# Residual loads and early stores of 4 MB instead of 2 MB, and a clear of the semaphores under the last stores, in a 3x3 convolution with a residual add

## The chip, the cores and the metric

One core of one Trainium2 chip. The metric is the device time of one execution in microseconds. A run is one execution; each comparison takes runs of both kernels in turn on the same chip.

## The reference

```python
batch, c_in, h, w, c_out, k = 16, 64, 64, 64, 64, 3
x_pad = np.pad(x, ((0, 0), (0, 0), (1, 1), (1, 1)))
for b, co, ci, kh, kw in ...:
    output[b, co] += weight[co, ci, kh, kw] * x_pad[b, ci, kh:kh+h, kw:kw+w]
return output + residual
```

`x`, `residual` and the output are 16 x 64 x 64 x 64 float32 each, 16.78 MB. An image of 64 channels fills 64 partitions, so two images, a pair, fill 128: 2.1 MB for each tensor and pair, called 2 MB here.

## The kernel before

The engines go by the names of the trace: PE is TensorE, DVE VectorE, ACT ScalarE, POOL GpSimd and SP SyncE. A DMA moves data between HBM, where the tensors lie, and SBUF, the core's working memory; PE writes its results to PSUM.

SP issues nearly all DMAs, in one order: x and residual of each pair alternately, then the stores. x comes into three buffers (`xr`), ACT casts it to bfloat16 (`xp`), PE makes 24 matmuls for each image, and DVE adds the result to the residual in place (`ro`, all eight pairs stay in SBUF). Of the eight stores six are issued inside the kernel's own block, when DVE has finished their pair; the last two come after it.

```python
    def load_ro(p):
        nc.sync.dma_start(out=ro[p][:, :], in_=res_bc[128 * p : 128 * p + 128, :]).then_inc(s_r[p], 16)
    ...
        for p in range(NPAIR):
            if p >= NXR:
                nc.sync.wait_ge(s_half, 2 * (p - NXR) + 3)        # ACT has emptied the x buffer
            if p == 0:
                to_the_front(load_x(p, cols=slice(0, NPIX // 2)))   # first half of x0, from SP
                nc.sync.dma_start(out=wraw[:, :], in_=w_rows[:, :]).then_inc(s_w, 16)
            else:
                load_x(p)
            load_ro(p)
        for p in range(NEARLY):                                     # NEARLY = 6
            nc.sync.wait_ge(s_add, 2 * p + 3)
            store(p).then_inc(s_out, 16)
    ...
        to_the_front(load_x(0, nc.scalar, slice(NPIX // 2, NPIX)))  # second half of x0, from ACT
    ...
    for p in range(NEARLY, NPAIR):
        store(p)
    with tc.tile_critical(sync_engine=mybir.EngineType.Pool, no_gpsimd_drain=True):
        nc.gpsimd.wait_ge(s_out, 16 * NEARLY)
```

Of the kernel before, what the change touches and what calls it, by code (L numbers as in the profile page):

```python
# [8 lines left out]
FP32 = mybir.dt.float32  # L9
# [6 lines left out]
def kernel(  # L16
# [7 lines left out]
    nc = tc.nc  # L24

    B, C, H, W = x.shape
# [4 lines left out]
    NPIX = H * W  # L31
    NPAIR = B // 2
# [2 lines left out]
    NCHUNK = J // JC  # L35
    NXR = 3
    NXP = 4
    NEARLY = 6

    res_bc = residual.rearrange("b c h w -> (b c) (h w)")  # L40
    out_bc = out.rearrange("b c h w -> (b c) (h w)")
    x_bc = x.rearrange("b c h w -> (b c) (h w)")
    w_rows = weight.rearrange("co (h ci) kh kw -> (co h) (ci kh kw)", h=2)

    pool = ctx.enter_context(tc.tile_pool(name="pool", bufs=1))
    psum = ctx.enter_context(tc.tile_pool(name="psum", bufs=1, space=bass.MemoryType.PSUM))

    ident = pool.tile([128, 128], FP32)
    ro = [pool.tile([128, NPIX], FP32, name=f"ro{p}") for p in range(NPAIR)]
    xr = [nc.alloc_sbuf_tensor(f"xr{i}", [128, NPIX], FP32) for i in range(NXR)]  # L50

    xp = [pool.tile([128, J + 1, W], BF16, name=f"xp{i}") for i in range(NXP)]
# [4 lines left out]
    sem = lambda name: tc.alloc_semaphore(name)  # L57
    s_w = sem("s_w")
    s_x = [sem(f"s_x{i}") for i in range(NXR)]
    s_r = [sem(f"s_r{p}") for p in range(NPAIR)]  # L60
    s_out = sem("s_out")
    s_id = sem("s_id")
    s_wt = sem("s_wt")
    s_half = sem("s_half")
    s_pack = sem("s_pack")
    s_bank = sem("s_bank")
    s_conv = sem("s_conv")
    s_add = sem("s_add")

    def load_x(p, engine=nc.sync, cols=slice(0, NPIX)):  # L70
        return engine.dma_start(out=xr[p % NXR][:, cols], in_=x_bc[128 * p : 128 * p + 128, cols]).then_inc(
            s_x[p % NXR], 16
        )

    def load_ro(p):
        nc.sync.dma_start(out=ro[p][:, :], in_=res_bc[128 * p : 128 * p + 128, :]).then_inc(s_r[p], 16)

    def store(p):
        return nc.sync.dma_start(out=out_bc[128 * p : 128 * p + 128, :], in_=ro[p][:, :])

    def matmul(out_, lhsT, rhs, start, stop, ldweights):

# [18 lines left out]
    def to_the_front(dma):  # L101



        def fixed(ap):
            t = ap.bass_ap.tensor.name
            return mybir.PhysicalAccessPattern(
                ap=ap.ap, offset=ap.bass_ap.offset, dtype=ap.dtype, memref=t, memsetref=t + "_set", bass_ap=ap.bass_ap
            )

        front = nc.main_func.blocks[0].instructions
        here = nc.cur_bb.bb.instructions
        ins = here.pop()
        assert ins.name == dma.ins.name
        at = next(
            i for i, e in enumerate(front) if e.engine == ins.engine and isinstance(e, mybir.InstDrain)
        )
        front.insert(at, copy.replace(ins, ins=[fixed(a) for a in ins.ins], outs=[fixed(a) for a in ins.outs]))
# [5 lines left out]
    def weight_block(h, half, d, par, kh):  # L124

        at = 64 * half + 32 * h
        return dict(out=wl[at : at + 32, d, :, par, :], in_=tp[0:32, kh, 0:384].rearrange("p (kw co h) -> p kw co h", kw=3, h=2)[:, :, :, h])

    with tc.tile_critical(no_gpsimd_drain=True):  # L129

        for p in range(NPAIR):
            if p >= NXR:

                nc.sync.wait_ge(s_half, 2 * (p - NXR) + 3)
            if p == 0:
                to_the_front(load_x(p, cols=slice(0, NPIX // 2)))
                nc.sync.dma_start(out=wraw[:, :], in_=w_rows[:, :]).then_inc(s_w, 16)
            else:
                load_x(p)
            load_ro(p)  # L140
        for p in range(NEARLY):
            nc.sync.wait_ge(s_add, 2 * p + 3)
            store(p).then_inc(s_out, 16)


        nc.gpsimd.memset(ident[:, :], 0.0).then_inc(s_id, 1)  # L146
        nc.gpsimd.wait_ge(s_id, 1)
        nc.gpsimd.affine_select(  # L148
            out=ident[:, :],
            in_=ident[:, :],  # L150
            compare_op=mybir.AluOpType.not_equal,
            fill=1.0,
            base=0,
            pattern=[[-1, 128]],
            channel_multiplier=1,
        ).then_inc(s_id, 1)
        nc.gpsimd.wait_ge(s_id, 2)
        for t in xp:
            nc.gpsimd.memset(t[0:64, 0, :], 0.0).then_inc(s_id, 1)  # L159
            nc.gpsimd.memset(t[64:128, J, :], 0.0).then_inc(s_id, 1)  # L160
        nc.gpsimd.memset(wl[0:64, 0, :, 1, :], 0.0).then_inc(s_id, 1)  # L161
        nc.gpsimd.memset(wl[64:128, 1, :, 0, :], 0.0).then_inc(s_id, 1)  # L162


        to_the_front(load_x(0, nc.scalar, slice(NPIX // 2, NPIX)))
        for n in range(B):
            p, im = divmod(n, 2)
            hp = slice(64 * im, 64 * im + 64)
            x4 = xr[p % NXR].rearrange("q (j two w) -> q j two w", two=2, w=W)
            t = xp[n % NXP]  # L170
            if im == 0:
                nc.scalar.wait_ge(s_x[p % NXR], 16 * (p // NXR + 1 + (p % NXR == 0)))
            i = nc.scalar.copy(out=t[64:128, 0:J, :], in_=x4[hp, :, 0, :])  # L173
            i.then_inc(s_half, 1)
            if n >= NXP:
                i._wait_ge(s_conv, n - NXP + 1)
            nc.scalar.copy(out=t[0:64, 1 : J + 1, :], in_=x4[hp, :, 1, :]).then_inc(s_pack, 1)  # L177
            if n == 0:
                nc.scalar.wait_ge(s_wt, 1)
                for b in blocks[4:]:  # L180
                    for h in range(2):
                        i = nc.scalar.copy(**weight_block(h, *b))  # L182
                i.then_inc(s_wt, 1)


        nc.vector.wait_ge(s_wt, 1)
        for k, b in enumerate(blocks[:4]):
            for h in range(2):
                i = nc.vector.tensor_copy(**weight_block(h, *b))  # L189
                if k == h == 0:  # L190
                    i.then_inc(s_bank, 2)
        i.then_inc(s_wt, 1)
        for n in range(B):
            p, im = divmod(n, 2)
            hp = slice(64 * im, 64 * im + 64)
            o4 = ro[p].rearrange("q (j two w) -> q j two w", two=2, w=W)
            psj = ps[n % 2].rearrange("q c j w -> q (c j) w")
            if im == 0:
                nc.vector.wait_ge(s_r[p], 16)
            for par in range(2):  # L200
                i = nc.vector.tensor_tensor(  # L201
                    out=o4[hp, :, par, :], in0=psj[64 * par : 64 * par + 64, :, :], in1=o4[hp, :, par, :], op=ADD
                )
                if par == 0:
                    i._wait_ge(s_conv, n + 1)

                i.then_inc(s_add if par == 0 or n == B - 1 else s_bank, 1)


        nc.tensor.wait_ge(s_id, 4 + 2 * NXP)  # L210
        nc.tensor.wait_ge(s_w, 16)
        wraw3 = wraw.rearrange("p (ci t) -> p ci t", t=9)
        for t in range(9):
            i = nc.tensor.transpose(  # L214
                out=tp[0:32, t // 3, 128 * (t % 3) : 128 * (t % 3) + 128], in_=wraw3[:, :, t], identity=ident[:, :]
            )
        i.then_inc(s_wt, 1)
        nc.tensor.wait_ge(s_wt, 3)
        with nc.Fori(0, B // NXP, 1, engines=[PE]):
            for n in range(NXP):  # L220
                nc.tensor.wait_ge(s_bank, 1).then_inc(s_bank, -1)
                nc.tensor.wait_ge(s_pack, 1).then_inc(s_pack, -1)  # L222
                order = [(1, 0), (1, 1), (0, 0), (0, 1), (2, 0), (2, 1)]
                for i, (kw, d) in enumerate(order):
                    xlo, xhi = max(0, 1 - kw), min(W, W + 1 - kw)
                    for c in range(NCHUNK):
                        j0 = JC * c
                        m = matmul(
                            ps[n % 2][:, c, :, xlo:xhi],
                            wl[:, d, kw, :, :].rearrange("q r c -> q (r c)"),  # L230
                            xp[n][:, j0 + d : j0 + d + JC, xlo + kw - 1 : xhi + kw - 1],
                            i == 0,
                            i == len(order) - 1,
                            c == 0,
                        )
                m.then_inc(s_conv, 1)


    for p in range(NEARLY, NPAIR):
        store(p)  # L240
    with tc.tile_critical(sync_engine=mybir.EngineType.Pool, no_gpsimd_drain=True):
        nc.gpsimd.wait_ge(s_out, 16 * NEARLY)


# [28 lines left out]
```

## Time and profile before

| what | value | from |
|---|---|---|
| time | 123.09 us (122.86 to 123.21, 3 runs) | the runs |
| span of the profiled run | 121.2 us | the page |
| DMA | 50.48 MB, 433 GB/s in most slices | the page |
| last add of DVE ends | 104.1 us | the timeline |
| last store has landed | 120.2 us | the landings |

The page is read with the DMA first, since those engines are the only ones busy from the first slice to the last. The prediction shows the lines. Two more are DVE's additions around image 4, in order of time: start, length of the run, how many, and in brackets how long DVE idled before it and for what.

```profile
37.27 4.61 DVE L201 TENSOR_TENSOR ro<-ps,ro 64x2048 f32<-64x2048 f32 x2 [0.58 <-PE ps L86]
42.46 4.61 DVE L201 TENSOR_TENSOR ro<-ps,ro 64x2048 f32<-64x2048 f32 x2 [0.58 <-PE ps L86]
```

Image 4, the first of pair 2, starts at 42.46 us, 0.58 us after the add before it, and what it waited for is PE.

### The profile page before, as it was taken

What the parts mean: (1) busy time and instruction counts of PE and PEld (TensorE: products, weight loads), DVE (VectorE), ACT (ScalarE), POOL (GpSimd) and SP (SyncE); (2) the same over time, 40 slices, a digit from 0 to 9 for tenths busy, and PEclk for the clock granted to TensorE, in tenths of its full rate; (3) what the DMA queues carried; (4) which work ended last, traced back from release to release, by engine and by line L of the source; (5) the groups of instructions that cost most, each with busy time, mean ns of one, the idle gap of its engine ahead of it and who ended that gap; (6) DMA issues with size and microseconds to landing.
All of it is one profiled execution on the core that took longest, in us unless ns stands there. A gap on an engine that the chain in (4) does not pass through costs nothing.

```text
span 121.2 us, 736 instructions
## 1 busy us (share of the span) xinstructions
PE 87.7 (72%) x389; PEld 10.7 (9%) x105; DVE 76.0 (63%) x40; ACT 63.1 (52%) x37; POOL 2.4 (2%) x16
## 2 busy tenths in 40 slices
PE   0033499999999999999999999999999980000000
PEld 0021001101010101010101010101010100000000
DVE  0005300889898898989889898898989889300000
ACT  4049969938966984993993994896000000000000
POOL 5200000000000000000000000000000000000000
PEclk9999999999999999999999999999999999755555
DMA  6999999999999999999999999999999999999993
GB/s 168 427 444 433 433 433 433 433 427 433 433 427 427 433 433 427 427 433 427 433 433 433 433 433 422 433 389 433 433 433 433 422 433 433 433 433 433 427 433 151
DMA packets 3744, 50.48 MB, mean 417 GB/s; under 512 B 416, under 2 KB 544, under 8 KB 544
## 3 DMA queue, kind: packets, MB, share of 16 engines
q1 hardware_dynamic: 3600, 49.43, 96.3%
q10 hardware_dynamic: 144, 1.05, 2.0%
HBM read 33.70 MB, written 16.78 MB: 417 GB/s over the span
## 4 chain that ended last, share of the span: by engine, by line
PE 71%; DVEq 2%; DVE 2%; issue 0%
PE ps L86 53%; PE ps L85 17%; DVEq L129 2%; DVE ro L201 2%
## 5 line engine op out<-in xcount | busy, mean ns | idle before, releaser
L201 DVE TENSOR_TENSOR ro<-ps,ro 64x2048 f32<-64x2048 f32 x32 | 73.2, 2289 | 17.7 <-PE ps L86 17.2
L86 PE MATMUL ps<-xp,wl 128*128 128x504 bf16 (+1 forms) x288 | 80.0, 388 | 0.2
L173 ACT CAST xp<-xr 64x2048 bf16<-64x2048 f32 x16 | 30.3, 1896 | 19.3 <-DMA xr<-in_x_dram 17.1
L85 PE MATMUL ps<-xp,wl 128*128 128x504 bf16 (+1 forms) x92 | 35.8, 389 | 3.4 <-PEq L222 3.4
L177 ACT CAST xp<-xr 64x2048 bf16<-64x2048 f32 x16 | 30.4, 1897 | 0.4
L85 PEld LDWEIGHTS ps<-xp,wl 128*128 128x128 bf16 x96 | 9.5, 99 | 79.1 <-issue 79.1
L189 DVE CAST wl<-ps 32x192 bf16<-32x192 f32 x8 | 2.8, 348 | 10.4 <-PE ps L214 10.3
L214 PE MATMUL ps<-ident,wraw 128*32 128x128 f32 x9 | 2.1, 412 | 8.1 <-DMA wraw<-in_weight_dram 8.1
L214 PEld LDWEIGHTS ps<-ident,wraw 128*32 128x32 f32 x9 | 1.2, 137 | 8.6 <-issue 8.1
L173 ACT ACT_TABLE_LOAD x1 | 1.3, 1283 | 1.1 <-SPq L129 1.1
L182 ACT CAST wl<-ps 32x192 bf16<-32x192 f32 x4 | 1.2, 306 | 0.0
L160 POOL MEMSET xp<- 64x64 bf16 x4 | 0.6, 147 | 0.2
L159 POOL MEMSET xp<- 64x64 bf16 x4 | 0.6, 145 | 0.2
L148 POOL TENSOR_SCALAR_AFFINE_SELECT ident<-ident 128x128 f32<-128x128 f32 x1 | 0.3, 295 | 0.2 <-POOL ident L146 0.2
L162 POOL MEMSET wl<- 64x192 bf16 x1 | 0.3, 253 | 0.1
L161 POOL MEMSET wl<- 64x192 bf16 x1 | 0.3, 252 | 0.1
L146 POOL MEMSET ident<- 128x128 f32 x1 | 0.2, 205 | 0.7 <-SPq L129 0.7
L257 POOL MEMSET const-uint8-127<- 128x1 uint8 x1 | 0.1, 113 | 0.0
L257 POOL MEMSET const-bfloat16-1.0<- 128x1 bf16 x1 | 0.1, 112 | 0.0
L257 POOL MEMSET const-float32-1.0<- 128x1 f32 x1 | 0.1, 109 | 0.0
L257 POOL MEMSET const-float32-0.0<- 128x1 f32 x1 | 0.1, 104 | 0.2 <-issue 0.2
## 6 DMA issues: line engine op xcount, KB each, us to landing
ro<-in_residual_dram SPq DMA_DIRECT2D x8, 2048.0 KB, 21.9
out_dram<-ro SPq DMA_DIRECT2D x8, 2048.0 KB, 28.2
xr<-in_x_dram SPq DMA_DIRECT2D x7, 2048.0 KB, 17.5
xr<-in_x_dram SPq DMA_DIRECT2D x1, 1024.0 KB, 7.0
xr<-in_x_dram ACTq DMA_DIRECT2D x1, 1024.0 KB, 7.6
wraw<-in_weight_dram SPq DMA_DIRECT2D x1, 144.0 KB, 6.9
```

Source lines behind the costliest of these rows:

```text
L85: return e.matmul(out=out_, lhsT=lhsT, rhs=rhs, start=start, stop=stop, skip_group_check=True)
L86: return e.add_instruction(mybir.InstMatmult(name=nc.get_next_instruction_name(), engine=PE, ins=[e.lower_ap(rhs), e.lower_ap(lhsT)], outs ...
L129: with tc.tile_critical(no_gpsimd_drain=True):
L159: nc.gpsimd.memset(t[0:64, 0, :], 0.0).then_inc(s_id, 1)
L160: nc.gpsimd.memset(t[64:128, J, :], 0.0).then_inc(s_id, 1)
L173: i = nc.scalar.copy(out=t[64:128, 0:J, :], in_=x4[hp, :, 0, :])
L177: nc.scalar.copy(out=t[0:64, 1 : J + 1, :], in_=x4[hp, :, 1, :]).then_inc(s_pack, 1)
L182: i = nc.scalar.copy(**weight_block(h, *b))
L189: i = nc.vector.tensor_copy(**weight_block(h, *b))
L201: i = nc.vector.tensor_tensor(out=o4[hp, :, par, :], in0=psj[64 * par : 64 * par + 64, :, :], in1=o4[hp, :, par, :], op=ADD)
L214: i = nc.tensor.transpose(out=tp[0:32, t // 3, 128 * (t % 3) : 128 * (t % 3) + 128], in_=wraw3[:, :, t], identity=ident[:, :])
L257: nc = _bacc.Bacc("TRN2", target_bir_lowering=False, num_devices=1)
```

## The change

Its intent: fewer and larger DMAs, fewer semaphores, and a clear of them while the last stores still run. (The split of the first load over both queues, which its short description also lists, is in the kernel before already.) The core of the diff:

```diff
-    NEARLY = 6
+    NEARLY = 3
+    RES = (slice(0, 1), slice(1, 2), slice(2, 4), slice(4, 6), slice(6, 8))
-    ro = [pool.tile([128, NPIX], FP32, name=f"ro{p}") for p in range(NPAIR)]
+    ro = pool.tile([128, NPAIR, NPIX], FP32)
-    s_r = [sem(f"s_r{p}") for p in range(NPAIR)]
+    s_r = [sem(f"s_r{i}") for i in range(2)]
-    s_wt = sem("s_wt")                       # its counts go to s_id
...
-    def load_ro(p):
-        nc.sync.dma_start(out=ro[p][:, :], in_=res_bc[128 * p : 128 * p + 128, :]).then_inc(s_r[p], 16)
+    def load_ro(i):
+        if i >= 2:
+            nc.sync.wait_ge(s_r[i % 2], 16 * (i // 2))
+        nc.sync.dma_start(out=ro[:, RES[i], :], in_=res_bc[:, RES[i], :]).then_inc(s_r[i % 2], 16)
...
-            load_ro(p)
-        for p in range(NEARLY):
-            nc.sync.wait_ge(s_add, 2 * p + 3)
-            store(p).then_inc(s_out, 16)
+            if p in (0, 1, 3, 5, 7):
+                load_ro((p + 1) // 2)
+        for k in range(NEARLY):
+            nc.sync.wait_ge(s_add, 4 * k + 5)
+            store(slice(2 * k, 2 * k + 2)).then_inc(s_out, 16)
...
         nc.gpsimd.wait_ge(s_out, 16 * NEARLY)
+        tc.free_semaphores([s_w, *s_x, *s_r, s_out, s_id, s_half, s_pack, s_bank, s_conv, s_add])
```

More of the change, by code (lines that the diff above doesn't have):

```diff
@@ L37 @@
     NXP = 4
-    NEARLY = 6
-    res_bc = residual.rearrange("b c h w -> (b c) (h w)")
-    out_bc = out.rearrange("b c h w -> (b c) (h w)")
+    NZERO = 4 + 2 * NXP
+    NEARLY = 3
+    RES = (slice(0, 1), slice(1, 2), slice(2, 4), slice(4, 6), slice(6, 8))
+    res_bc = residual.rearrange("(p b) c h w -> (b c) p (h w)", b=2)
+    out_bc = out.rearrange("(p b) c h w -> (b c) p (h w)", b=2)
     x_bc = x.rearrange("b c h w -> (b c) (h w)")
@@ L73, in load_x, with store @@
         )
-    def load_ro(p):
-        nc.sync.dma_start(out=ro[p][:, :], in_=res_bc[128 * p : 128 * p + 128, :]).then_inc(s_r[p], 16)
-    def store(p):
-        return nc.sync.dma_start(out=out_bc[128 * p : 128 * p + 128, :], in_=ro[p][:, :])
+    def load_ro(i):
+        if i >= 2:
+            nc.sync.wait_ge(s_r[i % 2], 16 * (i // 2))
+        nc.sync.dma_start(out=ro[:, RES[i], :], in_=res_bc[:, RES[i], :]).then_inc(s_r[i % 2], 16)
+    def store(pairs):
+        return nc.sync.dma_start(out=out_bc[:, pairs, :], in_=ro[:, pairs, :])
     def matmul(out_, lhsT, rhs, start, stop, ldweights):
@@ L178 @@
             if n == 0:
-                nc.scalar.wait_ge(s_wt, 1)
+                nc.scalar.wait_ge(s_id, NZERO + 1)
                 for b in blocks[4:]:
@@ L182 @@
                         i = nc.scalar.copy(**weight_block(h, *b))
-                i.then_inc(s_wt, 1)
-        nc.vector.wait_ge(s_wt, 1)
+                i.then_inc(s_id, 1)
+        nc.vector.wait_ge(s_id, NZERO + 1)
         for k, b in enumerate(blocks[:4]):
@@ L191 @@
                     i.then_inc(s_bank, 2)
-        i.then_inc(s_wt, 1)
+        i.then_inc(s_id, 1)
         for n in range(B):
@@ L195 @@
             hp = slice(64 * im, 64 * im + 64)
-            o4 = ro[p].rearrange("q (j two w) -> q j two w", two=2, w=W)
+            o4 = ro[:, p, :].rearrange("q (j two w) -> q j two w", two=2, w=W)
             psj = ps[n % 2].rearrange("q c j w -> q (c j) w")
             if im == 0:
-                nc.vector.wait_ge(s_r[p], 16)
+                i = next(i for i, pairs in enumerate(RES) if p < pairs.stop)
+                nc.vector.wait_ge(s_r[i % 2], 16 * (i // 2 + 1))
             for par in range(2):
@@ L207 @@
                 i.then_inc(s_add if par == 0 or n == B - 1 else s_bank, 1)
-        nc.tensor.wait_ge(s_id, 4 + 2 * NXP)
+        nc.tensor.wait_ge(s_id, NZERO)
         nc.tensor.wait_ge(s_w, 16)
@@ L216 @@
             )
-        i.then_inc(s_wt, 1)
-        nc.tensor.wait_ge(s_wt, 3)
+        i.then_inc(s_id, 1)
+        nc.tensor.wait_ge(s_id, NZERO + 3)
         with nc.Fori(0, B // NXP, 1, engines=[PE]):
@@ L236 @@
                 m.then_inc(s_conv, 1)
-    for p in range(NEARLY, NPAIR):
-        store(p)
+    for p in range(2 * NEARLY, NPAIR):
+        store(slice(p, p + 1))
     with tc.tile_critical(sync_engine=mybir.EngineType.Pool, no_gpsimd_drain=True):
         nc.gpsimd.wait_ge(s_out, 16 * NEARLY)
+        tc.free_semaphores([s_w, *s_x, *s_r, s_out, s_id, s_half, s_pack, s_bank, s_conv, s_add])
 _INS = ['x', 'weight', 'residual']
```

## The prediction

> **What bounds the kernel now.** I read the page first, its span, its slices and its DMA lines.
>
> ```profile
> span 121.2 us, 736 instructions
> DMA  6999999999999999999999999999999999999993
> ...
> DMA packets 3744, 50.48 MB, mean 417 GB/s; under 512 B 416, under 2 KB 544, under 8 KB 544
> ...
> q1 hardware_dynamic: 3600, 49.43, 96.3%
> ...
> HBM read 33.70 MB, written 16.78 MB: 417 GB/s over the span
> ...
> PE 71%; DVEq 2%; DVE 2%; issue 0%
> ```
>
> The reader is to see two things. The 16 DMA engines are busy in every slice but the first and the last. And the chain of waits (last line) names PE for 71% of the span; it misleads here, because it follows compute instructions back from the last add, and that add ends long before the span does. What ends the span is the store of the last pair. The stretches show it:
>
> ```profile
> 1.00:20.00 19.00, 8.42 (x27) 1.80 (x14) 2.78 (x8) 12.19 (x11) 2.17 (x12) 1.00 1.01 414
> 20.00:78.00 58.00, 57.84 (x267) 6.54 (x67) 50.16 (x22) 45.07 (x24) 0.00 (x0) 1.00 1.01 431
> 78.00:80.00 2.00, 2.00 (x11) 0.19 (x2) 1.42 (x2) 1.98 (x2) 0.00 (x0) 1.00 0.99 352
> 80.00:104.00 24.00, 19.43 (x90) 2.14 (x22) 21.53 (x10) 3.87 (x3) 0.00 (x0) 1.00 1.00 430
> 104.00:119.00 15.00, 0.00 (x0) 0.00 (x0) 0.13 (x1) 0.00 (x0) 0.00 (x0) 0.51 1.01 433
> 119.00:121.20 2.20, 0.00 (x0) 0.00 (x0) 0.00 (x0) 0.00 (x0) 0.00 (x0) 0.50 0.09 37
> ```
>
> Columns: the stretch, its length, busy time of PE, weight loads, DVE, ACT and POOL, granted clock, DMA share, GB/s. From 104 to 119 us no compute engine works, and the DMA engines still run at share 1.01 and 433 GB/s on stores queued before. So the end is set by bytes divided by rate.
>
> The span divides by the trace's packet and landing records like this. The first load is issued at 0.00 and its first packet starts at 1.01. Packets then run until 119.87. The last store's semaphore lands at 120.21, and the final barrier, with the clearing of semaphores, ends at 121.17. That is 1.01 + 118.86 + 0.34 + 0.96 = 121.17 us. The packets' own durations add up to 119.1 us for each of the 16 engines, so there is no idle time to win inside the 118.86: what is busy is the wire. A 16 KB packet takes 608 at best, 611 in the median and 613 ns in the mean (16 x 16,384 B / 611 ns = 429 GB/s). Only the end of an engine's list is uneven: the 16 engines finish between 119.3 and 119.9.
>
> The tail's costs, from the line of the framework's exit code, and the DMA queue's waits:
>
> ```profile
> L268 POOLq EVENT_SEMAPHORE_RANGE_CLEAR  x1: 200/200/200, 120.7 to 120.7; - x1
> ```
>
> ```profile
> SPq L71 <- ACT xp L173: 51.4, 5, 15.7
> SPq L79 <- DVE ro L201: 24.9, 4, 10.0
> SPq L129 <- DVEq L129: 17.4, 1, 17.4
> SPq L268 <- DMA out_dram<-ro: 14.8, 2, 10.0
> ```
>
> The clear is one instruction of 0.2 us. SP waits for nearly the whole span, but the DMA engines have work queued meanwhile, so these waits cost nothing.
>
> **What the Trainium skill says.** Page "DMA: Bandwidth & Descriptors", section "Where 436 GB/s comes from", gives 16 ports x 32 B x 850 MHz = 435.2 GB/s as the ceiling of one core's DMA. The trace agrees: 433 GB/s in most slices, so the steady state is within 1% of it. Section "Measured (HBM→SBUF, 128 partitions, SWDGE, issued from GpSimd)" gives 78% efficiency for 1 MB and 97% for 16 MB and advises large DMAs. That is for a transfer timed by itself; this trace doesn't agree for queued ones: its 2 MB transfers, back to back, already run at 433. Section "Why a DMA increments its semaphore by 16 and not by 1" says that each engine closes a DMA with a semaphore descriptor and that two DMAs in flight on one semaphore let a wait pass early. The trace has 416 four-byte packets, 16 for each of 26 DMAs, 9 ns each; and the second point is why the changed kernel makes SP wait before it issues a residual load on a reused semaphore. Section "Latency and other measured facts" lists row pitches of 2 MiB as slow (164 GB/s against 207 and more). In the changed kernel a partition's two rows are 2 MiB apart, but neighbouring partitions stay 16 KB apart, so I don't expect that case; no line of the kernel before tests it.
>
> **The change part by part.** The first part of its name, the load split over both queues, is in the kernel before too: both kernels issue one 1 MB half from SP and one from ACT at 0.0 and 0.13 us. Nothing moves there.
>
> (1) Residual loads go from eight of 2 MB to 2, 2, 4, 4, 4 MB, early stores from six of 2 MB to three of 4 MB. Bytes are the same and a row is still 16 KB, so the large packets are the same 2,944 of 16 KB. Six fewer DMAs (26 to 20: three loads and three stores) remove 6 x 16 = 96 semaphore packets of 9 ns over 16 engines: 96 x 9 / 16 = 54 ns. SP's six issues of about 0.43 us were hidden.
>
> (2) The order of the queue changes: x3 comes before the residual of pair 2, which now comes with pair 3's, and so on; all loads still precede all stores. I walked the queue with 4.87 us for each 2 MB (the distance of the landings before). Loads before landed at: x2 27.5, ro2 32.3, x3 37.2, ro3 42.1. After: x2 27.5, x3 32.4, residuals of pairs 2 and 3 together 42.1. DVE's first add for pair 2 (image 4) started at 42.46, so the residual arrives 0.4 us before it is needed. The next two come at 61.6 (needed at 63.2) and 81.3 (needed at 84.0). Should the first be late by d, the compute chain, where PE takes 24 matmuls x 216 ns = 5.19 us for each image with hardly any slack against DVE (2 x 2.29 us and 0.58 of wait), ends d later than 104.1.
>
> (3) Does the queue ever run dry? x5 waits for image 6's first cast, after x3: issued at about 37, while queued work reaches to 47. x7 and the last residual load are issued at about 57, with work to 66. The 4 MB stores wait for images 4, 8 and 12, at 57 (behind the loads), 65.5 and 86.3 us; the last of these is the same moment as the sixth small store before, and work then reaches to 100.8. The stores of pairs 6 and 7 are issued after the last add, at 104.4 before, while stores queued earlier run until 110; an issue takes 1.0 us to its first packet, so they may come some 4.5 us later at no cost. No gap opens.
>
> (4) Semaphores. The program of the changed kernel keeps the clear at the very end and adds a second one ahead of it: the final one covers 22 numbers (29 before), the added one 13. The added one waits for the early stores and, by the framework's own waits, for pair 6's store (landed 115.4). It costs some 0.2 us of POOL and is done by about 116, under pair 7's store, which lands at 120.2: hidden. What is saved is at most the shorter range of the final clear. If its 200 ns were all proportional to the count, 200 x 7/29 = 48 ns; if it is fixed, nothing. I take half, 25 ns. The two barriers around it stay.
>
> Sum: 54 + 25 = about 0.08 us, under 0.1% of 123.09. Predicted 123.0.
>
> **Rivals.** First, a transfer that gets more efficient: 4 MB transfers could take packets from 613 to the best 608 ns. Over 2,944 / 16 = 184 packets for each engine that is 0.9 us, 122.1. For it: 352 GB/s in the dip at 78 to 80. Against: the median packet is at 611 already, only 28 packets of over 640 ns make the dip, they cost 0.36 us on the average engine, and they lie inside one load, not at boundaries between DMAs.
>
> Second, a wait in place of the removed: the grouped residual comes late and holds DVE, then PE. For it: only 0.4 us of room at image 4. Against: 4.5 us of room before the last stores. Even 2 us late would leave the time at 123.0; 6 us late would cost about 1.5, 124.5.
>
> Third, slower transfers, because a partition's two rows lie 2 MiB apart: 5% on the 25.2 MB moved so (3 loads and 3 stores of 4.19 MB) would be 25.2 / 433 x 0.05 = 2.9 us, 126. For it only the skill's row; against it, that neighbours keep their 16 KB pitch[...].
>
> Fourth, the whole clear leaves the tail, with its barrier: 0.6 us, 122.5. Against: the final clear and both barriers are still in the built program.
>
> **Range and chances.** The three runs before lie within 0.35 us (122.86 to 123.21), and a dip like that at 78 us can come or go (0.36). With the gain of 0.08 that gives 122.6 to 123.4. Faster by 2% would need 2.46 us, which no part of the sum nor any rival but a faster wire reaches: 2%. Slower by 2% needs the third rival: 2%. The rest, 96%, is within.
>
> **What would show it.** Right: span near 121.1; DMA share 1.0 from 1 us to the last slice; 3,648 packets; 2 MB per 4.87 us at the landings; the last add at 104 to 105; one clear near 116 and one near 120.7, the latter at 150 to 200 ns. Step (2) is wrong if DVE waits for a residual load before image 4 by more than a few tenths; step (3), if a slice before the last falls below 9; step (4), if the distance from last landing to end leaves 0.96 by more than 0.1. The prediction as a whole is wrong if the large packets' mean leaves 611 to 615 ns.

## The result, and the profile after

The changed kernel takes 122.92 us (122.79 to 123.03, 6 runs) against 123.12 us (122.86 to 123.3, 6 runs): ratio 0.9985, 95% interval 0.9971 to 0.9999. A ratio is the mean time of one kernel's runs over that of the other's of the same rounds, so it is not quite the ratio of the medians quoted. Executions over 1.5% slower than the fastest of the same kernel are left out of the means. Against the 123.0 predicted this is 0.08 us off, inside the range.

The page of the changed kernel:

```profile
span 121.1 us, 735 instructions
...
DMA  6999999999999999999999999999999999999992
...
DMA packets 3648, 50.48 MB, mean 417 GB/s; under 512 B 320, under 2 KB 448, under 8 KB 448
...
q1 hardware_dynamic: 3504, 49.43, 96.1%
...
HBM read 33.70 MB, written 16.78 MB: 417 GB/s over the span
...
PE 43%; DVEq 2%; DVE 2%; issue 0%
```

The packets are the 3,648 that were worked out, the bytes and the mean rate are unchanged, and the DMA engines are busy in every slice but the first and the last, as before. The chain names PE for 43% instead of 71%. This is no improvement of PE: the chain is followed back from the last add, and it now breaks where that add's forerunners waited for a DMA. Here is that place, DVE in order of time:

```profile
35.99 4.61 DVE L206 TENSOR_TENSOR ro<-ps,ro 64x2048 f32<-64x2048 f32 x2 [0.58 <-PE ps L89]
42.25 9.25 DVE L206 TENSOR_TENSOR ro<-ps,ro 64x2048 f32<-64x2048 f32 x4 [1.65 <-DMA ro<-in_residual_dram]
```

DVE idled 1.65 us for the grouped residual of pairs 2 and 3, which landed at 42.2. Before, the same image waited for PE until 42.46. In `after_again`, the same kernel in another run, it did so too, and there the chain names PE for 71% again:

```profile
42.43 4.61 DVE L206 TENSOR_TENSOR ro<-ps,ro 64x2048 f32<-64x2048 f32 x2 [0.57 <-PE ps L89]
```

The stretches of the changed kernel (columns as in the prediction):

```profile
20.00:78.00 58.00, 57.17 (x265) 6.43 (x66) 50.35 (x22) 47.10 (x25) 0.00 (x0) 1.00 1.01 432
78.00:80.00 2.00, 2.00 (x11) 0.29 (x3) 1.53 (x1) 1.63 (x2) 0.00 (x0) 1.00 1.01 393
80.00:104.00 24.00, 19.18 (x89) 2.05 (x21) 21.36 (x10) 2.27 (x2) 0.00 (x0) 0.95 1.00 430
104.00:119.00 15.00, 0.00 (x0) 0.00 (x0) 0.00 (x0) 0.00 (x0) 0.00 (x0) 0.50 1.01 431
```

From 104 to 119 us no compute engine works and the DMA engines still run at share 1.01. And the two clears, by the kernel's own line and by the framework's exit line:

```profile
L248 POOLq EVENT_SEMAPHORE_RANGE_CLEAR  x1: 113/113/113, 115.8 to 115.8; - x1
```

```profile
L274 POOLq EVENT_SEMAPHORE_RANGE_CLEAR  x1: 153/153/153, 120.7 to 120.7; - x1
```

The added clear ends at 115.9 us, under the last store. The final one takes 153 ns instead of 200. From the last landing to the end it is 0.90 us instead of 0.96 (121.127 - 120.231 against 121.172 - 120.213, from the landings in the traces). From the first packet to the last it is 118.87 us in both.

### The profile page after: what moved, and what is told of

Same layout as the page of the kernel before. It is cut to its first block, busy times and chain, and to the rows that moved or that the text cites. A ratio compares the mean times of both kernels' runs of the same rounds, so it can differ in the third digit from the quotient of the medians.

```text
span 121.1 us, 735 instructions
## 1 busy us (share of the span) xinstructions
PE 86.7 (72%) x393; PEld 10.6 (9%) x105; DVE 76.0 (63%) x40; ACT 63.1 (52%) x37; POOL 2.4 (2%) x16
## 2 busy tenths in 40 slices
DMA packets 3648, 50.48 MB, mean 417 GB/s; under 512 B 320, under 2 KB 448, under 8 KB 448
## 6 DMA issues: line engine op xcount, KB each, us to landing
out_dram<-ro SPq DMA_DIRECT2D x2, 2048.0 KB, 13.5
```

## The experiments

Twelve kernels ran, in three groups, each beside the kernel before on its chip.

### The whole change again, and each part alone

`after_again` and `after_third` are the changed kernel unchanged. `merge_only` leaves out its last line; `clear_only` is the kernel before with such a line alone:

```diff
# merge_only, on the changed kernel
-        tc.free_semaphores([s_w, *s_x, *s_r, s_out, s_id, s_half, s_pack, s_bank, s_conv, s_add])
# clear_only, on the kernel before
+        tc.free_semaphores([s_w, *s_x, *s_r, s_out, s_id, s_wt, s_half, s_pack, s_bank, s_conv, s_add])
```

> The changed kernel once more, as the control for the three beside it. My theory (same bytes at the same rate, only 54 ns of semaphore packets and about 47 ns of final clear saved): ratio 0.999, between 0.9975 and 1.0; span 121.1. The rival that a large packet got cheaper says the mean 16 KB packet stays at 612 against 613 ns before in every pair of profiles; mine says this mean wanders by about 1 ns either way.

Measured: 123.12 us against 123.16, ratio 1.0001 (0.9987 to 1.0015). So the repetition did not show the gain.

> The changed kernel a third time, to pool with 0.9985 and 1.0001: between 0.998 and 1.001. Its tail from the last landing to the end is 0.90 us, as in both profiles of it so far.

Measured: 122.94 us against 123.07, ratio 0.9987 (0.9972 to 1.0002). The mean of the three ratios is 0.9991, 0.11 us; two of the three intervals hold 1. A gain of about 0.1 us fits, and nothing finer can be said.

> The changed kernel without the clear under the stores. The final clear still covers 22 numbers instead of 29. My theory: nothing is lost against the changed kernel, ratio to before 0.999 (0.9975 to 1.0), final clear 153 ns, GpSimd done earlier by about 0.2 us near 116 us. Rival (the overlapped clear is what saves time): ratio back at 1.000 and a longer distance from the last landing to the end (0.96 instead of 0.90 us).

Measured: ratio 1.0001 (0.9988 to 1.0015), the same as `after_again` in the same rounds; both lie just above the 0.9975 to 1.0 that I expected. The profiled final clear took 158 ns and the tail was 0.905 us: the shorter tail is there without the clear under the stores.

> The kernel before with only the clear under the stores added. The final clear still covers 29 numbers. My theory: ratio 1.000 (0.999 to 1.001), final clear 200 ns, tail 0.96 us, the added clear some 0.15 us near 116 us. Rival (the overlapped clear shortens the tail): tail under 0.85 us and ratio 0.998 or less.

Measured: ratio 1.0004 (0.999 to 1.0017), tail 0.95 us. Its two clears:

```profile
L243 POOLq EVENT_SEMAPHORE_RANGE_CLEAR  x1: 139/139/139, 116.0 to 116.0; - x1
```

```profile
L269 POOLq EVENT_SEMAPHORE_RANGE_CLEAR  x1: 196/196/196, 120.9 to 120.9; - x1
```

The added clear at 116.0 costs 139 ns that nobody waits for, and the final one keeps its 196 ns, since it still covers all 29 numbers. So the clear under the stores saves nothing in either form. What shortens the tail is having fewer semaphores.

### What a semaphore costs at the end

```diff
# many_sems, on the changed kernel
+    s_more = [sem(f"s_more{i}") for i in range(60)]
```

> The changed kernel with 60 unused semaphores more, so that the final clear covers 82 numbers instead of 22. If the clear costs time by the number (29: 200 ns, 22: 153 ns, 13: 113 ns give 4.4 to 6.7 ns each), it takes 420 to 560 ns, the tail grows by 0.26 to 0.40 us and the ratio to before is 1.001 to 1.002. If the clear costs a fixed time and 153 against 200 was chance, it stays at 150 to 200 ns and the ratio at 0.999.

Measured: 123.53 us, ratio 1.0031 (1.0018 to 1.0045), against 1.0001 of the changed kernel in the same rounds. This is above the 1.001 to 1.002 that I expected.

```profile
L275 POOLq EVENT_SEMAPHORE_RANGE_CLEAR  x1: 478/478/478, 121.0 to 121.0; - x1
```

The clear grew with the number, by (478 - 153) / 60 = 5.4 ns for each. The tail grew from 0.896 to 1.302 us, 6.8 ns for each: the rest is a drain ahead of the clear, 169 ns instead of 88. The seven semaphores that the change saves are thus worth 7 x 6.8 = 47 ns, and 63 were seen. This one term goes straight into the time, because at that point all engines wait in a barrier.

### What a DMA costs in a full queue

`halves` is the kernel before with each 2 MB DMA in two by columns:

```diff
# halves, on the kernel before (stores and x loads in the same way)
     def load_ro(p):
-        nc.sync.dma_start(out=ro[p][:, :], in_=res_bc[128 * p : 128 * p + 128, :]).then_inc(s_r[p], 16)
+        for cols in HALVES:
+            nc.sync.dma_start(out=ro[p][:, cols], in_=res_bc[128 * p : 128 * p + 128, cols]).then_inc(s_r[p], 16)
```

> The kernel before with every 2 MB DMA issued as two of 1 MB by columns: 49 DMAs instead of 26, rows of 8 KB instead of 16. My theory (a DMA costs the queue only its 16 semaphore packets of 9 ns): 23 x 9 ns = 0.2 us for the semaphores, and two 8 KB packets at 309 ns against one of 611 give 7 ns x 2,944 / 16 = 1.3 us; together 1.5 us, ratio 1.012 (1.005 to 1.016). Rival (each DMA costs its landing of 0.34 us or more, so that merging should have saved 6 x 0.34 = 2 us): 23 x 0.34 = 7.8 us, ratio 1.06, with gaps in the DMA share.

Measured: 123.65 us against 123.17, ratio 1.0036 (1.0017 to 1.0055), under the range that I expected.

```profile
span 122.0 us, 760 instructions
...
DMA  6999999999999999999999999999999999999993
...
DMA packets 7056, 50.48 MB, mean 414 GB/s; under 512 B 784, under 2 KB 912, under 8 KB 912
```

```profile
20.00:78.00 58.00, 57.84 (x267) 6.54 (x67) 49.95 (x22) 44.45 (x24) 0.00 (x0) 1.00 1.01 427
80.00:104.00 24.00, 19.63 (x91) 2.15 (x22) 21.53 (x10) 4.57 (x3) 0.00 (x0) 1.00 1.02 429
104.00:119.00 15.00, 0.00 (x0) 0.00 (x0) 0.33 (x1) 0.00 (x0) 0.00 (x0) 0.53 1.01 427
```

The engines stay full, at 427 to 429 GB/s. The rival, a landing paid for each DMA, is off by a factor of over fifteen. My own figure was also too high: it added up durations, and packets' durations overlap. Their sum for each engine is 120.3 us here, in a stretch of 119.5 us. So 23 DMAs more and packets of half the size cost 0.44 us together (0.0036 x 123.17), which leaves some 19 ns for each DMA and 0.12 us for the six that the change saves, if the smaller packets cost nothing (29 ns and 0.18 us at the upper end of the interval).

### How late a residual may come

Three kernels put the residuals of pair 2 and later further back, each by one change on the changed kernel:

```diff
# late_inside: half of x4 goes ahead of the residuals of pairs 2 and 3 (its other half follows; ACT waits for both)
+            if p == 3:
+                nc.sync.wait_ge(s_half, 2 * (p + 1 - NXR) + 3)
+                load_x(p + 1, cols=slice(0, NPIX // 2))
# late_edge: 6 MB loads, issued after x3 and x6
-    RES = (slice(0, 1), slice(1, 2), slice(2, 4), slice(4, 6), slice(6, 8))
+    RES = (slice(0, 1), slice(1, 2), slice(2, 5), slice(5, 8))
# late_over: one 8 MB load after x3, the last after x7
+    RES = (slice(0, 1), slice(1, 2), slice(2, 6), slice(6, 8))
```

> The changed kernel with the residuals of pairs 2 to 7 in two 6 MB loads, so that pair 2's residual lands at 47.0 us instead of 42.1. My theory: DVE waits some 6 us before image 4, the last add ends at about 108.7 instead of 104, the last two stores are issued near 109 with 1.0 us to their first packet, and stores queued before run until 110.1: no or nearly no gap, ratio 0.998 to 1.003. Rival (a late residual reaches the end of the kernel one for one): about 4.5 us more, ratio 1.037.

Measured: 124.7 us against 123.17, ratio 1.0103 (1.0058 to 1.0149), 1.3 us in place of nearly nothing.

```profile
span 123.3 us, 730 instructions
...
PEclk9999999999999999557999999999999999995555
DMA  6999999999999999999999999999999999957993
GB/s 178 423 447 425 441 436 425 431 436 425 431 436 425 441 425 431 431 425 431 441 425 436 431 425 436 377 420 425 425 425 425 441 441 436 431 234 335 431 425 170
```

```profile
46.87 9.25 DVE L206 TENSOR_TENSOR ro<-ps,ro 64x2048 f32<-64x2048 f32 x4 [5.00 <-DMA ro<-in_residual_dram]
59.59 4.61 DVE L206 TENSOR_TENSOR ro<-ps,ro 64x2048 f32<-64x2048 f32 x2 [3.48 <-PE ps L89]
```

Two things are to be seen. First, the DMA engines have a gap now, in the slice that reads 234 GB/s (from 107.9 us; a slice is 3.08 us) and the next. Second, DVE waits 5.00 us for the residual, as planned, but then again 3.48 us for PE before image 6, where 0.58 us is usual. The clock line tells why: it falls to 5 tenths in the slices from 49 to 55 us. PE's matmuls in that place:

```profile
46.78 0.81 PE L89 MATMUL ps<-xp,wl 128*128 128x504 bf16 x3
52.15 1.48 PE L89 MATMUL ps<-xp,wl 128*128 128x512 bf16 x3 [4.55 <-PEq L227]
...
57.01 0.81 PE L89 MATMUL ps<-xp,wl 128*128 128x504 bf16 x3
```

Each record there is a run of matmuls. PE stood for 4.55 us, because both halves of PSUM were full; three matmuls after that took 1.48 us, and 0.81 us from 57 us on. The Trainium skill's page "TensorE: Matmul & The Clock Gate", section "Part 1: The HAM clock gate (the "warmup" mystery)", states that the array goes back to half its clock after an idle window of about 3.4 us and needs as long a busy one to leave it. The trace agrees in the main: after this stand PE ran for some 4.6 us at the slow pace. No exact threshold can be read from these runs: the recorded clock fell 2.3 us after the last matmul here, 5.1 us after it in `late_over`, and not at all in the 2.4 us that PE stood in `late_inside`. Of DVE's 3.48 us some 2.4 are the slow clock, for `late_inside`, which did not cool, has 1.04 us before the same image. So the last add ended at 110.9, not at the 108.7 expected. That is 6.8 us later than the 104.1 of before, and the profiled end came 2.1 us later (123.3 against 121.2): a room of 4.7 us. (The profiled run was the slowest of its four, 125.08 us of 124.0 to 125.08, so it shows more than the 1.3 us of the ratio.)

> The same with the residuals of pairs 2 to 5 in one 8 MB load, which lands at 51.8 us. My theory: the last add ends at about 113.5, beyond the room of 4.5 us; the DMA engines go idle for about 4.6 us near 111 to 115, the time is 123.0 + 4.6 = 127.6, ratio 1.037 (1.025 to 1.045). If the end did not depend on the last add, it would stay at 1.000.

Measured: 130.13 us, ratio 1.0544 (1.0504 to 1.0583). The direction is as expected and the size over the range, again by the cooling: the wait of 10.41 us was followed by one of 3.89 us for PE.

```profile
GB/s 186 427 437 439 433 428 423 444 433 418 439 439 428 418 444 439 413 439 439 423 143 270 439 439 408 388 418 423 428 449 413 433 444 428 423 71 245 408 459 194
```

The DMA engines ran low twice: at the end (71 and 245), as expected, and already near 66 us (143 and 270). The late residual had also held back the loads: x7 waits for ACT's cast of image 10, which waits for PE to finish image 6, and so it was issued at 66.8 us, when x6 had all but landed (67.0). The last add ended at 116.15, 12.0 us later than before, and the end came 7.36 us later (128.53 against 121.17): 12.03 - 7.36 is a room of 4.7 us again. The first gap does not show in the end, which comes 12.38 us after the last add in both late kernels.

> The changed kernel with half of x4 loaded ahead of the residuals of pairs 2 and 3, which then land at 44.6 us instead of 42.2: late, but meant to stay inside the room before the last stores. After the first two late runs my theory is: DVE waits 2 to 4 us before image 4, PE cools in that wait or not (0 to 2.9 us more at image 6), the last add ends at 106 to 109, stores queued before run to 110.1 and the next need an issue by about 109: ratio 0.999 to 1.003, against 1.03 if lateness went through one for one.

Measured: 122.84 us against 123.07, ratio 0.9983 (0.9966 to 1.0).

```profile
44.49 9.25 DVE L211 TENSOR_TENSOR ro<-ps,ro 64x2048 f32<-64x2048 f32 x4 [3.03 <-DMA ro<-in_residual_dram]
54.78 2.28 DVE L211 TENSOR_TENSOR ro<-ps,ro 64x2048 f32<-64x2048 f32 x1 [1.04 <-PE ps L89]
```

DVE idles 3.03 us for the residual. PE's wait behind it was 2.4 us, it did not cool (1.04 us before image 6), and the last add ended at 106.1, two microseconds later than before. Nothing of this reaches the time.

### Is it bytes?

```diff
# skip_store, on the changed kernel; the output of pair 0 is wrong on purpose
-            store(slice(2 * k, 2 * k + 2)).then_inc(s_out, 16)
+            store(slice(2 * k + (k == 0), 2 * k + 2)).then_inc(s_out, 16)
```

> The changed kernel without the store of pair 0 (its output is wrong on purpose). My theory (bytes at the rate of the DMA engines set the end): 2.1 MB less is 4.87 us less, less a gap of 0 to 0.3 us since the last stores are then issued just as the queue ends: ratio 0.960 to 0.963. Rival (the chain of waits, with PE at most of it, sets the end): ratio 0.995 or more.

Measured: 118.12 us against 123.17, ratio 0.9596 (0.957 to 0.9621): 4.98 us less (0.0404 x 123.17), where 2.1 MB at the distance of landings are 4.87. The ratio is just under the 0.960 to 0.963 expected, whose lower part lies in the interval. Compute is unchanged (last add at 103.6). The end follows the bytes.

### The first load, and a second queue

```diff
# unsplit, on the changed kernel (ACT's wait counts one DMA less)
-                to_the_front(load_x(p, cols=slice(0, NPIX // 2)))
+                to_the_front(load_x(p))
-        to_the_front(load_x(0, nc.scalar, slice(NPIX // 2, NPIX)))
# two_queues, on the changed kernel: SP keeps the first and third early store
+        nc.scalar.wait_ge(s_add, 9)
+        store(slice(2, 4), nc.scalar).then_inc(s_out, 16)
```

> The changed kernel with the first load as one 2 MB DMA from SP (which both kernels have split over SP and ACT). My theory: bytes set the end, so nothing: ratio to before 0.998 to 1.001. One DMA fewer and 128 rows of 16 KB for 256 of 8 KB are worth under 0.05 us. Rival (the split starts the DMA engines or the chain of compute sooner and that reaches the end): 0.2 us or more, ratio 1.001 to 1.003.

Measured: 122.79 us against 123.07, ratio 0.998 (0.9965 to 0.9995). The split that both kernels carry buys nothing here. The kernel is not slower without it; that it would be faster than the changed one is not shown, 0.9987 in the same rounds with an interval that covers it.

> The changed kernel with the second 4 MB store issued from ACT, so that two queues feed the DMA engines from about 84 to 110 us; an attempt at a kernel faster than both. If a second queue fills what is left between packets, the 16 KB packets of this stretch come closer than 611 ns and up to 0.3 us is won, ratio 0.996 to 0.997. My theory: the engines have no gaps to fill, ratio 0.998 to 1.001, and 433 GB/s at most in any stretch.

Measured: 122.9 us, ratio 0.9989 (0.9975 to 1.0003). The stretch with both queues at work, and the one after it:

```profile
84.00:104.00 20.00, 15.16 (x70) 1.66 (x17) 18.00 (x8) 0.00 (x0) 0.00 (x0) 1.00 1.00 429
104.00:119.00 15.00, 0.00 (x0) 0.00 (x0) 0.00 (x0) 0.00 (x0) 0.00 (x0) 0.51 1.00 430
```

429 and 430 GB/s: no gap was there to fill. No version was found that clearly beats both kernels. The experiments say why: as long as the queue holds work, the time between first and last packet follows the bytes, and reordering or regrouping them moves it by tenths of a microsecond.

## Why the prediction was right

The number alone says little: an effect of 0.1 us stands in a range of 0.8 us, and any forecast of no change would have hit it. What the runs test is the steps.

**What sets the end.** Right: without one store the kernel is 4.98 us shorter, while PE, ACT and DVE do the same work.

**(1) Fewer DMAs, 54 ns.** Not contradicted, and not measured by itself: from `halves` the six DMAs are worth some 0.12 us, 0.18 at the upper end. The first packet to the last took 118.87 us in both of the first profiles, and between 118.87 and 119.07 in three profiles of the changed kernel. That spread hides 54 ns. One remark of this step was loose: the durations of packets add up to more than the time they take, so "119.1 us busy" in 118.86 us was overlap, not a measure of fullness to the last tenth.

**(2) The order of the queue.** The landing was right: 42.1 predicted, 42.2 measured, and 61.6 and 81.3 for the next two, as predicted. That DVE would not need it before 42.46 was an assumption from one profile. DVE's first add came at 20.4 us in the changed kernel's first profile and at 21.7 before; in it DVE waited 1.65 us. This differs between executions of one kernel. In all three profiles of the changed kernel PE began its first image at 13.5 to 13.8 us with slow matmuls, 1.48 us for three; they took 0.81 us from 16.4 us on in the first profile, from 17.3 in `after_third` and from 18.9 in `after_again`. With its first add at 20.7 us DVE waited 1.09 us for the residual (`after_third`), with it at 21.7 not at all (`after_again`). In the three profiles of kernels with the old order the fast pace came at 19.0 to 19.5 us; whether the change moves it is open. By the criterion that I had put down, this step failed. It cost nothing: the last add ended at 103.8, earlier than before, and `late_inside` shows that even 106.1 is free. The prediction had this in its second rival: even 2 us late would leave the time at 123.0. The step's other half, that a delay of d ends d later, held here: the wait was 1.07 us longer than usual, and from first add to last it took 83.40 us instead of 82.41. But it lacked a term: the 4.55 us for which PE stood in `late_edge` brought back the slow clock, which cost some 2.4 us more (3.48 against 1.04 in `late_inside`).

**(3) The queue never runs dry.** Right for the changed kernel. The room of "some 4.5 us" measured 4.7 us in each of the two kernels that overran it.

**(4) Semaphores.** The mechanism was right, the clear under the stores is hidden and what counts is the range of the final clear. The size was off: I halved 48 ns for want of knowledge. The clear grows by 5.4 ns for each number, on some 34 ns that stay (153 - 22 x 5.4); 47 ns were saved in it, and 63 ns of tail with the drain ahead of it.

**The rivals.** Cheaper packets: the mean of 16 KB packets was 613.0 ns before and 612.1, 612.9 and 613.5 in three profiles of the changed kernel, so no. Slower packets because of rows 2 MiB apart: no, by the same numbers. The clear leaving the tail with its barrier: no, `clear_only` keeps its tail at 0.95 us. The late residual is discussed above.

What remains open is how much of the three ratios (0.9985, 1.0001, 0.9987) is the 0.06 us of tail and how much chance. In all profiles but that of `halves` some 16 KB packets of over 640 ns (up to 1,171 ns before) stand some 2 us before the loads end, near 79 us where they end near 81. They cost 0.1 to 0.6 us on the average engine and differ between profiles of the same kernel (0.17, 0.34 and 0.45 us in three of the changed one, with spans of 121.1, 121.3 and 121.3). (`halves` has 8 KB packets instead, and none of them took over 338 ns between 70 and 90 us; their median is 309.) They may be a source of the scatter, which is argued, not shown. Against it stands that `two_queues`, with 0.31 us of them, took 118.78 us from first packet to last, and `clear_only`, with 0.28, took 119.07.

## What to carry to other kernels

When the DMA engines are full from the first packet to the last, joining 2 MB transfers into 4 MB ones moves only their boundaries, and those cost tens of nanoseconds: look for bytes to leave out, or for time before the first packet and after the last. A late input is free as long as the queue behind it holds work for longer than the delay; work out this room before reordering, and add the price of a TensorE that cools in the wait (2.4 us here) and of loads that wait behind it. To clear semaphores early saves nothing as long as a final clear covers the same numbers again; to allocate fewer saves some 7 ns each.

## What the Trainium skill lacked or had wrong

- No page gives what the range clear in a kernel's own exit costs by the number of semaphores. Runs here: 113 ns for 13 numbers, 139 for 20, 153 to 158 for 22, 196 to 203 for 29, 478 for 82; the tail grows by 6.8 ns for each.
- "DMA: Bandwidth & Descriptors", section "Measured (HBM→SBUF, 128 partitions, SWDGE, issued from GpSimd)", advises to batch and lists 78% for a transfer of 1 MB. That doesn't carry over to a full queue: 49 DMAs, nearly all of 1 MB, ran at 427 to 429 GB/s, 98% of the page's 435, and cost 0.44 us more than 26 DMAs. A price for one more DMA in a full queue is what the page lacks; here it is some 19 ns, 29 at the upper end.
- The same page's section "Latency and other measured facts" lists 2 MiB row pitches as slow. It doesn't say that a pitch of 2 MiB between two rows of one partition, with 16 KB between partitions, is harmless: 16 KB packets took 612 to 613.5 ns so, 613.0 without.
- No page tells of slow packets ahead of the turn from loads to stores: 16 KB packets of up to 1,415 ns instead of 611, 0.1 to 0.6 us on the average engine.
